# Padded tiles so that both operands of a split matmul start at a multiple of 128 bytes

## Chip, cores and metric

One core of a Trainium2 chip runs the kernel. The metric is device time in microseconds (us) of one execution; three runs of the kernel before gave a median of 1478.23 us (1478.17 to 1478.27).

## What is computed

A decoder layer on 256 tokens of width 2048, in float32: one input projection of 14,848 columns, retention with four heads, sliding-window attention with 32 query heads and a sink, two gates, an output projection, a layer norm, a SwiGLU feed-forward of width 5632 and a second layer norm. Cut to what matters here:

```python
proj = h @ w_in[l]
...
merged = jax.nn.sigmoid(gate_a) * ret + jax.nn.sigmoid(gate_b) * att
h = layer_norm(DEEPNORM_ALPHA * h + merged @ w_out[l], ln1_g[l], ln1_b[l])
ffn = (jax.nn.silu(h @ w_gate[l]) * (h @ w_up[l])) @ w_down[l]
h = layer_norm(DEEPNORM_ALPHA * h + ffn, ln2_g[l], ln2_b[l])
```

## The kernel before

**Split matmuls.** Every large product is done in the type `float32r`. Each float32 operand is split into a rounded high part and the rest: ScalarE casts a weight block `raw` to `wh` (L188), VectorE subtracts to get `wl` (L189), and three matmuls per tile stand for one (L204 to L206):

```python
nc.tensor.matmul(self.acc[t], lhsT=xh, rhs=wh[:, j], start=st, stop=False)
nc.tensor.matmul(self.acc[t], lhsT=xh, rhs=wl[:, j], start=False, stop=False)
nc.tensor.matmul(self.acc[t], lhsT=xl, rhs=wh[:, j], start=False, stop=sp)
```

`lhsT` is the stationary operand: 128 columns, loaded by an LDWEIGHTS of its own that the profile books on PEld. `rhs` is the moving operand: 512 columns. There is one LDWEIGHTS for each matmul, and it is issued one matmul ahead. Names as the profile prints them: `acc<-wh,xh` is moving `wh`, stationary `xh`.

**Stages.** The class `Chunk` walks one block of 512 output columns over all k; `Stream` puts the chunks behind each other and starts loads and casts ahead. In order of time:

- input projection, 29 chunks of 16 k-tiles by two token tiles, stationary `xh`/`xl` (the split input). The first chunk (moving `wh1`/`wl1` in the code, printed as `wh`/`wl`) loads the input along with its weights. Attention, retention and gates run between its steps as background jobs: transposes (L492), scores (L539, L606) and values (L568, L632), all plain float32 matmuls;
- output projection, 4 chunks, stationary `mh`/`ml`; then the first layer norm;
- gate and up projection: two chunks (`Chunk`, L204 to L206), then ten `PairChunk`s (L294 to L296), stationary `hh`/`hl`. A `PairChunk` also uses sums of its operands: stationary `sh`/`sl`, moving `th`/`tl`. In each, three groups of 12 matmuls with moving `th`/`tl` stand between groups with moving `wh`/`wl`;
- down projection in three parts, 12 chunks, stationary `ph`/`pl`, placed after every fourth `PairChunk` or so; then the second layer norm and the store.

The order on each engine is the order of the code: `Stream.run` issues one step of matmuls, then `pump` lets background jobs go one step.

**Where tiles lie.** Tile pools take SBUF as two stacks, a left one that grows up and a right one (`side=RIGHT`) that grows down from the top; each tile is rounded up to 32 bytes per partition and nothing else aligns it. The left stack begins at 16512 bytes, a multiple of 128. `const` puts 1056 bytes (`cst`) and 32 (`halfpi`) there, so everything behind it is 64 bytes off a multiple of 128; in `xp` three tables of 1088 bytes bring `xh` and what follows back to a multiple. The right stack begins 32 bytes under the top, so all its tiles, whose sizes are multiples of 128, start 96 bytes past a multiple. That gives, from the layout of the built program, in bytes past a multiple of 512:

| operands (moving / stationary) | split matmuls | before | after |
|---|---|---|---|
| `wh1`,`wl1` / `xh`,`xl` (first chunk) | 96 | 32 / 0 | 0 / 384 |
| `wh`,`wl` / `xh`,`xl` | 2304 | 192 / 0 | 384 / 384 |
| `wh`,`wl` / `mh`,`ml` | 384 | 192 / 480 | 384 / 384 |
| `wh`,`wl` / `hh`,`hl`,`sh`,`sl` | 1662 | 192 / 192 | 384 / 384 |
| `th`,`tl` / `hh`,`hl`,`sh`,`sl` | 360 | 480 / 192 | 384 / 384 |
| `wh`,`wl` / `ph`,`pl` | 1056 | 192 / 480 | 384 / 384 |

The step from one slice of a tile to the next (`wh[:, j]`, `xh[:, k]`, a token tile) is a multiple of 512 bytes, so a tile has one such value for all its slices.

Of the kernel before, what the change touches and what calls it, by code (L numbers as in the profile page):

```python
# [9 lines left out]
F32 = mybir.dt.float32  # L10
F32R = mybir.dt.float32r
I32 = mybir.dt.int32
AF = mybir.ActivationFunctionType
ALU = mybir.AluOpType
RIGHT = "right"

P = 128
# [36 lines left out]
    "215db93af8c88f39c4105f38a7072d37"  # L54
)
NFR = 136


def _split_const(v, grid, parts):
# [34 lines left out]
def layer_kernel(ctx, tc, a, out):  # L94
    nc = tc.nc
    PS = bass.MemoryType.PSUM

    const = ctx.enter_context(tc.tile_pool(name="const", bufs=1))
    rawp = ctx.enter_context(tc.tile_pool(name="raw", bufs=3))
    spl = ctx.enter_context(tc.tile_pool(name="spl", bufs=NSPL))  # L100
    psc = ExitStack()
# [37 lines left out]
    class Chunk:  # L139
# [25 lines left out]
        def dma(self, b):  # L165
            k, n = self.blocks[b]
            if self.src is None:
                x_dma(b)
                self.raw[b] = xraw[b][:, :, SEQ:]
                return  # L170
            r = rawp.tile([P, KB, C], F32, name="raw")
            if n == KB:
                nc.sync.dma_start(out=r, in_=self.src[k // KB])
            else:
                o = k % KB
                nc.sync.dma_start(out=r[:, 0:n], in_=self.src[k // KB][:, o:o + n])
            self.raw[b] = r
# [175 lines left out]
    jobs = {}  # L353

    NC0 = P + NFR
    cst = const.tile([P, NC0], F32, name="cst")
    ident = cst[:, 0:P]
    freq = cst[:, P:NC0]
    halfpi = const.tile([P, 1], F32, name="halfpi")
    nc.gpsimd.memset(halfpi, math.pi / 2)  # L360

    def bcast_cols(dram, c0, n):
# [13 lines left out]
    xp = inp.enter_context(tc.tile_pool(name="xp", bufs=1))  # L376
# [1 line left out]
    dmask = msk[:, 0:RH * 384].rearrange("p (h c) -> p h c", h=RH)  # L378
    bmask = msk[:, RH * 384:]
    sinks = xp.tile([P, NH], F32, name="sinks")  # L380
    cosr = xp.tile([P, 2, NFR], F32, name="cosr")
    sinr = xp.tile([P, 2, NFR], F32, name="sinr")
    sinn = xp.tile([P, 2, NFR], F32, name="sinn")
    xh = xp.tile([P, KT, SEQ], F32R, name="xh")
    xl = xp.tile([P, KT, SEQ], F32R, name="xl")
    att = xp.tile([P, 2, DM], F32, name="att")
# [5 lines left out]
    ini = isc.enter_context(tc.tile_pool(name="ini", bufs=1))  # L392
# [9 lines left out]
    xraw = {}  # L402

    def x_dma(b):
        k = sum(XS[:b])
        r = ini.tile([P, max(XS), SEQ + C], F32, name="xraw", bufs=XB)
        nc.sync.dma_start(out=r[:, 0:XS[b]], in_=a["xw"][:, k:k + XS[b]])
        xraw[b] = r
        if b == 2:
            nc.scalar.dma_start(out=cst, in_=a["consts"][:, 0:NC0])  # L410
            xraw["pos"] = ini.tile([P, 2], I32, name="posi")
            nc.scalar.dma_start(out=xraw["pos"], in_=a["pos"])

    def x_cast(b):
# [9 lines left out]
    def tables():  # L424
        posi = xraw["pos"]
        posf = ini.tile([P, 2], F32, name="posf")
        nc.vector.tensor_copy(out=posf, in_=posi)
        ang = ini.tile([P, 2, NFR], F32, name="ang")
        for t in range(2):
            nc.vector.tensor_scalar(out=ang[:, t], in0=freq, scalar1=posf[:, t:t + 1], scalar2=None, op0=ALU.mult)  # L430
        yield
        SH = [P, 2, NFR]
        cur = ang
# [40 lines left out]
        yield  # L474

    def rot_small(x16, t, n):
        # x16: [P, n, 2, 8]
        sh = [P, n, 2, 8]
        t1 = ap_.tile([P, n, 2, 8], F32, name="ra")
        t2 = ap_.tile([P, n, 2, 8], F32, name="rb")  # L480
        cs = cosr[:, t, 128:136].unsqueeze(1).unsqueeze(1).broadcast_to(sh)
        sp = sinr[:, t, 128:136].unsqueeze(1).broadcast_to([P, n, 8])
        sn = sinn[:, t, 128:136].unsqueeze(1).broadcast_to([P, n, 8])
        nc.vector.tensor_mul(out=t1, in0=x16, in1=cs)
        nc.vector.tensor_mul(out=t2[:, :, 0], in0=x16[:, :, 1], in1=sn)
        nc.vector.tensor_mul(out=t2[:, :, 1], in0=x16[:, :, 0], in1=sp)
        nc.vector.tensor_add(out=x16, in0=t1, in1=t2)
# [12 lines left out]
    def akv_bg():  # L500
        for _ in range(AKD):
            yield
        for t in range(2):
            rot_small(kvt[:, t, 0:256].rearrange("p (h d) -> p h d", d=HD)[:, :, 0:16].rearrange("p h (a b) -> p h a b", a=2), t, NKV)
            kd = ap_.tile([P, NKV, 2, HD], F32, name="kd")
            kv_ = kvt[:, t, 0:256].rearrange("p (h d) -> p h d", d=HD)
            for u in range(2):
                nc.vector.tensor_copy(out=kd[:, :, u], in_=kv_)
            yield
            ps = transpose4([kd[:, g].rearrange("p a d -> p (a d)") for g in range(NKV)])  # L510
            yield
            nc.scalar.copy(out=kT[:, :, t * P:(t + 1) * P], in_=ps)
            yield
# [5 lines left out]

    def attention(g, t, q):  # L520
        rot_small(q.rearrange("p (h d) -> p h d", d=HD)[:, :, 0:16].rearrange("p h (a b) -> p h a b", a=2), t, 8)
        yield
        ps = transpose4([q[:, i * P:(i + 1) * P] for i in range(4)])
# [157 lines left out]
    n = 0  # L681
# [12 lines left out]
        inchunk(n, lambda ch, t, j=j: gate(ch, t, j, "b")); n += 1  # L694
    mark_b = len(stream.steps)

    # out projection
    sc = {}

    def lhs_m(k, t):  # L700
# [178 lines left out]
            stream.add(Chunk([a["w_down"][c, f0 + b] for b in range(nk // KB)], nk, lhs_p, lambda ch, t, part=part, c=c: done_d(ch, t, part, c),  # L879
                             order=stagger(NSPL) if part == 2 and c == 3 else None))  # L880

    # ---- run
    i = 0
    for b, n in enumerate(XS):
        stream.precast[i] = lambda b=b: x_cast(b)
# [27 lines left out]
    hp = fsc.enter_context(tc.tile_pool(name="hp", bufs=1))  # L913
# [5 lines left out]
    sc["hl"] = hp.tile([P, KT, SEQ], F32R, name="hl")  # L919
    sc["sh"] = hp.tile([P, 4, NQ, P], F32R, name="sh")  # L920
    sc["sl"] = hp.tile([P, 4, NQ, P], F32R, name="sl")
    sc["stats"] = hp.tile([P, 2, 4, 6], F32, name="stats1")
    nc.sync.dma_start(out=sc["hres"], in_=a["x"].rearrange("(t p) d -> p t d", p=P))
    gains = {}
    for nm in ("ln1_g", "ln1_b"):
# [13 lines left out]
    psc.close()  # L939
    p8 = ctx.enter_context(tc.tile_pool(name="p8", bufs=8, space=PS, reuse_waits="tile"))  # L940
    psp["all"] = p8
    sc["stats"] = hp.tile([P, 2, 4, 6], F32, name="stats2")
    stream.run(mark_e, PC)
    for nm, tg in (("ln2_g", "hh"), ("ln2_b", "hl")):
        gains[nm] = hp.tile([P, DM], F32, name=tg)
# [79 lines left out]
```

## Time and profile before

| | us |
|---|---|
| median of three runs | 1478.23 |
| span of the profiled execution, first to last instruction | 1476.8 |
| TensorE busy in it | 1460.0 (99%) |
| VectorE busy | 962.6 (65%) |
| ScalarE busy | 654.7 (44%) |
| granted TensorE clock, mean | 0.996 of full |

The profile records the span of its execution and no total beside it; 1.4 us lie between the span and the median of the runs. A matmul's end is modelled in the profile and neighbours overlap in it (one of 0.39 us starts every 0.23 us), so what a matmul costs is read from the distance between two starts, which is called its pace here. A busy TensorE alone doesn't say whether it could go faster.

### The profile page before, as it was taken

How to read it: one execution, taken by the hardware profiler on the slowest of the kernel's cores; microseconds unless marked ns; L12 is line 12 of the kernel's file. 1: busy time of each engine (PE TensorE's matmuls, PEld its weight loads, DVE VectorE, ACT ScalarE, POOL GpSimd, SP SyncE). 2: the span in 40 equal slices, each digit the busy share in tenths (PEclk: the TensorE clock that was granted, in tenths of full speed). 3: DMA queues.
4: the chain of work that ended last, by engine and by line, in shares of the span. 5: the costliest groups of instructions: out<-in, count | busy, mean ns of one | idle time of the engine just before them, and what ended most of it. 6: DMA issues, size and time to landing. Idle time of an engine off the chain costs nothing.

```text
span 1476.8 us, 15948 instructions
## 1 busy us (share of the span) xinstructions
PE 1460.0 (99%) x6562; PEld 1177.8 (80%) x6562; DVE 962.6 (65%) x1011; ACT 654.7 (44%) x617; POOL 0.9 (0%) x6
## 2 busy tenths in 40 slices
PE   8999999999999999999999999999999999999997
PEld 6878888878788787788877888888888888888885
DVE  8455555454555545555598887457998755798756
ACT  6464543343443434443354554344455433454431
POOL 0000000000000000000000000000000000000000
PEclk9999999999999999999999999999999999999998
DMA  8643334555555455575455555555555555655561
GB/s 295 234 145 125 115 115 143 197 176 186 181 201 173 172 197 172 179 276 208 163 183 205 186 206 190 174 196 199 206 194 190 188 192 182 217 185 214 193 222 69
DMA packets 40232, 274.73 MB, mean 186 GB/s; under 512 B 4704, under 2 KB 4832, under 8 KB 8160
## 3 DMA queue, kind: packets, MB, share of 16 engines
q1 hardware_dynamic: 39296, 272.53, 52.6%
q10 hardware_dynamic: 864, 1.19, 0.2%
q8 instruction: 51, 0.84, 0.2%
q14 instruction: 21, 0.17, 0.0%
HBM read 271.60 MB, written 2.10 MB: 185 GB/s over the span
## 4 chain that ended last, share of the span: by engine, by line
PE 97%; DVE 2%; DMA 0%; issue 0%; ACT 0%; DVEq 0%; ACTq 0%
PE acc L204 15%; PE acc L206 15%; PE acc L205 15%; PE bank L294 9%; PE bank L296 9%; PE bank L295 9%; PE bank L204 6%; PE bank L206 6%; PE bank L205 6%; PE tr L492 2%; PE mx L568 1%; PE mx L539 1%; DVE wl L189 1%; PE bank L492 1%; PE mx L632 0%; DVE hres L724 0%
## 5 line engine op out<-in xcount | busy, mean ns | idle before, releaser
L189 DVE TENSOR_TENSOR wl<-raw,wh 128x2048 fp32r<-128x2048 f32 x164 | 375.7, 2291 | 318.7 <-ACT wh L188 318.3
L188 ACT CAST wh<-raw 128x2048 fp32r<-128x2048 f32 x164 | 313.2, 1910 | 454.5 <-PE acc L206 249.9
L204 PE MATMUL acc<-wh,xh 128*128 128x512 f32 x800 | 321.5, 403 | 1.8 <-ACT wh L188 1.8
L205 PE MATMUL acc<-wl,xh 128*128 128x512 f32 x800 | 318.9, 399 | 0.5 <-DVE wl L189 0.5
L206 PE MATMUL acc<-wh,xl 128*128 128x512 f32 x800 | 317.4, 397 | 0.0
L274 ACT CAST wh<-raw 128x1536 fp32r<-128x1536 f32 (+1 forms) x80 | 140.4, 1755 | 129.5 <-PE bank L296 78.5
L275 DVE TENSOR_TENSOR wl<-raw,wh 128x1536 fp32r<-128x1536 f32 (+1 forms) x80 | 166.5, 2088 | 26.7 <-ACT wh L274 25.9
L204 PEld LDWEIGHTS acc<-wh,xh 128*128 128x128 f32 x800 | 150.8, 189 | 40.3 <-ACT wh L188 3.2
L205 PEld LDWEIGHTS acc<-wl,xh 128*128 128x128 f32 x800 | 150.7, 188 | 37.6 <-issue 2.2
L294 PE MATMUL bank<-wh,hh 128*128 128x512 f32 x460 | 180.4, 392 | 0.0
L206 PEld LDWEIGHTS acc<-wh,xl 128*128 128x128 f32 x800 | 150.6, 188 | 37.4 <-issue 1.3
L296 PE MATMUL bank<-wh,hl 128*128 128x512 f32 x460 | 179.3, 390 | 0.0
L295 PE MATMUL bank<-wl,hh 128*128 128x512 f32 x460 | 178.9, 389 | 0.0
L204 PE MATMUL bank<-wh,ph 128*128 128x512 f32 x352 | 139.5, 396 | 0.0
L206 PE MATMUL bank<-wh,pl 128*128 128x512 f32 x352 | 139.2, 395 | 0.0
L205 PE MATMUL bank<-wl,ph 128*128 128x512 f32 x352 | 139.2, 395 | 0.0
L296 PEld LDWEIGHTS bank<-wh,hl 128*128 128x128 f32 x460 | 86.3, 188 | 18.8
L295 PEld LDWEIGHTS bank<-wl,hh 128*128 128x128 f32 x460 | 86.4, 188 | 18.2
L294 PEld LDWEIGHTS bank<-wh,hh 128*128 128x128 f32 x460 | 86.3, 188 | 17.9
L274 ACT CAST th<-tsum 128x2048 fp32r<-128x2048 f32 x30 | 57.5, 1915 | 53.8 <-DVE tsum L262 34.9
L275 DVE TENSOR_TENSOR tl<-tsum,th 128x2048 fp32r<-128x2048 f32 x30 | 68.8, 2292 | 16.0 <-ACT th L274 16.0
L206 PEld LDWEIGHTS bank<-wh,pl 128*128 128x128 f32 x352 | 66.1, 188 | 16.0
(187 smaller groups left out, 1489.0 us busy)
## 6 DMA issues: line engine op xcount, KB each, us to landing
raw<-in_w_in SPq DMA_DIRECT2D x96, 1024.0 KB, 4.9
raw<-in_w_gu SPq DMA_DIRECT2D x88, 1024.0 KB, 5.0
raw<-in_w_down SPq DMA_DIRECT2D x44, 1024.0 KB, 5.0
raw<-in_w_out SPq DMA_DIRECT2D x16, 1024.0 KB, 5.0
xraw<-in_xw SPq DMA_DIRECT2D x7, 768.0 KB, 5.7
hres<-in_x SPq DMA_DIRECT2D x1, 2048.0 KB, 7.6
gg<-in_gn_g SPq DMA_DIRECT2D x4, 256.0 KB, 3.7
gb<-in_gn_b SPq DMA_DIRECT2D x4, 256.0 KB, 3.7
```

The source lines that it names most:

```text
L188: nc.scalar.copy(out=h[:, 0:m], in_=r)
L189: nc.vector.tensor_sub(out=l[:, 0:m], in0=r, in1=h[:, 0:m].bitcast(F32))
L204: nc.tensor.matmul(self.acc[t], lhsT=xh, rhs=wh[:, j], start=st, stop=False)
L205: nc.tensor.matmul(self.acc[t], lhsT=xh, rhs=wl[:, j], start=False, stop=False)
L206: nc.tensor.matmul(self.acc[t], lhsT=xl, rhs=wh[:, j], start=False, stop=sp)
L274: nc.scalar.copy(out=h_, in_=r)
L275: nc.vector.tensor_sub(out=l_, in0=r, in1=h_.bitcast(F32))
L294: nc.tensor.matmul(self.acc[p], lhsT=xh, rhs=wh[:, j], start=st, stop=False)
L295: nc.tensor.matmul(self.acc[p], lhsT=xh, rhs=wl[:, j], start=False, stop=False)
L296: nc.tensor.matmul(self.acc[p], lhsT=xl, rhs=wh[:, j], start=False, stop=sp)
L492: nc.tensor.transpose(ps[:, i], s, ident)
L539: nc.tensor.matmul(sps[u][:, i], lhsT=qT[u * HD:(u + 1) * HD, h // 2], rhs=kT[u * HD:(u + 1) * HD, g, 0:W], start=True, stop=True)
```

## The change

No instruction is added, removed or moved, and no wait is: both programs have the same 9,143 instructions in the same order with the same waits. Tiles of odd width get padding, so that every later tile of a pool starts at a multiple of 128 bytes: `cst` 264 to 288 columns, `halfpi` 1 to 32, the three rotary tables 136 to 144 columns, `posi` 2 to 32, the statistics of the layer norms 6 to 8 columns. A tile `edge` of 96 bytes that nobody uses is put at the top of the right stack. Three Sin activations now write 2x136 where they wrote 272 elements, and four BN_AGGR read 4x6 where they read 24.

```diff
+LINE = 32
+NFL = 144
...
     const = ctx.enter_context(tc.tile_pool(name="const", bufs=1))
+    edge = ctx.enter_context(tc.tile_pool(name="edge", bufs=1, side=RIGHT))
+    edge.tile([P, LINE - 8], F32, name="edge")
...
-    cst = const.tile([P, NC0], F32, name="cst")
+    cst = const.tile([P, LINE * -(-NC0 // LINE)], F32, name="cst")
...
-    halfpi = const.tile([P, 1], F32, name="halfpi")
+    halfpi = const.tile([P, LINE], F32, name="halfpi")[:, 0:1]
...
-    cosr = xp.tile([P, 2, NFR], F32, name="cosr")
-    sinr = xp.tile([P, 2, NFR], F32, name="sinr")
-    sinn = xp.tile([P, 2, NFR], F32, name="sinn")
+    cosr = xp.tile([P, 2, NFL], F32, name="cosr")[:, :, 0:NFR]
+    sinr = xp.tile([P, 2, NFL], F32, name="sinr")[:, :, 0:NFR]
+    sinn = xp.tile([P, 2, NFL], F32, name="sinn")[:, :, 0:NFR]
...
-            nc.scalar.dma_start(out=cst, in_=a["consts"][:, 0:NC0])
-            xraw["pos"] = ini.tile([P, 2], I32, name="posi")
+            nc.scalar.dma_start(out=cst[:, 0:NC0], in_=a["consts"][:, 0:NC0])
+            xraw["pos"] = ini.tile([P, LINE], I32, name="posi")[:, 0:2]
...
-    sc["stats"] = hp.tile([P, 2, 4, 6], F32, name="stats1")
+    sc["stats"] = hp.tile([P, 2, 4, 8], F32, name="stats1")[:, :, :, 0:6]
...
-    sc["stats"] = hp.tile([P, 2, 4, 6], F32, name="stats2")
+    sc["stats"] = hp.tile([P, 2, 4, 8], F32, name="stats2")[:, :, :, 0:6]
```

Two comment lines are dropped as well, and the added lines shift the numbers of the lines behind them.

## Rows read from the trace of the kernel before

**Rows 1.** The page's busy time of each engine, and engines of the chain.

```profile
PE 1460.0 (99%) x6562; PEld 1177.8 (80%) x6562; DVE 962.6 (65%) x1011; ACT 654.7 (44%) x617; POOL 0.9 (0%) x6
...
PE 97%; DVE 2%; DMA 0%; issue 0%; ACT 0%; DVEq 0%; ACTq 0%
```

**Rows 2.** Waits of TensorE: line, releaser, us in total, times, longest.

```profile
PE acc L204 <- ACT wh L188: 1.8, 1, 1.8
...
PE acc L205 <- DVE wl L189: 1.0, 2, 0.5
```

**Rows 3.** Groups of matmuls by shape: count, busy us, mean ns, idle us.

```profile
L206 PE MATMUL acc<-wh,xl 128*128 128x512 f32 x800 | 317.4, 397 | 0.0
...
L296 PE MATMUL bank<-wh,hl 128*128 128x512 f32 x460 | 179.3, 390 | 0.0
...
L206 PE MATMUL bank<-wh,pl 128*128 128x512 f32 x352 | 139.2, 395 | 0.0
...
L206 PE MATMUL acc<-wh,ml 128*128 128x512 f32 x128 | 50.6, 395 | 0.0
...
L296 PE MATMUL bank<-th,sl 128*128 128x512 f32 x90 | 35.6, 395 | 0.0
...
L296 PE MATMUL bank<-th,hl 128*128 128x512 f32 x30 | 11.9, 397 | 0.0
...
L296 PE MATMUL bank<-wh,sl 128*128 128x512 f32 x30 | 11.7, 389 | 0.0
```

**Rows 4.** The same groups from 420 to 460 us, in the input projection.

```profile
L205 PE MATMUL acc<-wl,xh 128*128 128x512 f32 x58 | 22.9, 396 | 0.0
L206 PE MATMUL acc<-wh,xl 128*128 128x512 f32 x58 | 22.9, 396 | 0.0
L204 PE MATMUL acc<-wh,xh 128*128 128x512 f32 x57 | 22.5, 395 | 0.0
```

**Rows 5.** The same groups from 762 to 788 us, in the up projection's `Chunk`.

```profile
L205 PE MATMUL acc<-wl,hh 128*128 128x512 f32 x39 | 15.2, 389 | 0.0
L206 PE MATMUL acc<-wh,hl 128*128 128x512 f32 x39 | 15.2, 389 | 0.0
L204 PE MATMUL acc<-wh,hh 128*128 128x512 f32 x38 | 14.8, 389 | 0.0
```

**Rows 6.** Timeline of TensorE in a `PairChunk`: start us, us, instruction.

```profile
802.60 0.39 PE L294 MATMUL bank<-wh,hh 128*128 128x512 f32 x1
...
804.41 0.39 PE L296 MATMUL bank<-wh,sl 128*128 128x512 f32 x1
804.64 0.40 PE L294 MATMUL bank<-th,sh 128*128 128x512 f32 x1
...
807.21 0.40 PE L296 MATMUL bank<-th,hl 128*128 128x512 f32 x1
807.44 0.40 PE L294 MATMUL bank<-wh,hh 128*128 128x512 f32 x1
...
809.07 0.39 PE L295 MATMUL bank<-wl,hh 128*128 128x512 f32 x1
```

**Rows 7.** Timeline of TensorE around eight transposes, next `PairChunk`.

```profile
865.88 0.48 PE L294 MATMUL bank<-wh,hh 128*128 128x512 f32 x1
866.19 0.40 PE L295 MATMUL bank<-wl,hh 128*128 128x512 f32 x1
...
866.88 0.39 PE L295 MATMUL bank<-wl,hh 128*128 128x512 f32 x1
```

**Rows 8.** Timeline of all engines at 800 us: a matmul and the next weight load.

```profile
800.79 0.39 PE L295 MATMUL bank<-wl,hh 128*128 128x512 f32 x1
800.79 0.19 PEld L296 LDWEIGHTS bank<-wh,hl 128*128 128x128 f32 x1
```

**Rows 9.** Stretches: us, busy PE, PEld, DVE, ACT, POOL, clock, DMA share, GB/s.

```profile
9.00:42.00 33.00, 32.51 (x135) 25.81 (x134) 32.06 (x61) 22.40 (x24) 0.00 (x0) 0.96 0.86 319
42.00:648.60 606.60, 606.41 (x2830) 486.98 (x2829) 323.73 (x432) 267.23 (x335) 0.00 (x0) 1.00 0.49 168
...
742.00:790.00 48.00, 46.94 (x213) 37.47 (x212) 44.03 (x54) 23.08 (x24) 0.00 (x0) 1.00 0.56 197
792.00:916.00 124.00, 123.47 (x549) 101.18 (x548) 101.01 (x82) 61.26 (x43) 0.00 (x0) 1.00 0.55 196
```

## Prediction

> **What bounds the kernel now.** I read the page first. TensorE is busy 99% of the span and takes 97% of the chain that ended last; VectorE has 65% and ScalarE 44% [rows 1]. The view of waits says why that share is not hiding stalls: in the whole run TensorE's longest entry is one wait of 1.8 us, at the start, and the next is 1.0 us in two pieces [rows 2]. So the time is the number of matmuls times their pace, and only a change of the pace or of the count can move it by much. This change leaves the count alone.
>
> Does the pace depend on where operands lie? The trace of before holds the comparison, since its tiles lie at different offsets. By groups, a split matmul is booked with 389 to 390 ns where moving `wh` meets stationary `hl` or `sl`, and with 395 to 397 ns where `wh` meets `xl`, `ml` or `pl`, or `th` meets `sl` or `hl` [rows 3]. Ends are modelled, so I check with starts. From 420 to 460 us, 173 matmuls touch the window [rows 4]. The first may have begun up to 0.396 us before it, so their pace is about 40.4/173 = 0.2335 us. From 762 to 788 us it is 26.4/116 = 0.2275 us [rows 5]. Both stretches run at the full granted clock, the higher of the two levels [rows 9].
>
> These are different stages, so the timeline inside one `PairChunk` matters more. From the start at 802.60 to that at 804.64 are nine matmuls with moving `wh`/`wl`: 2.04/9 = 0.2267 us. From 804.64 to 807.44 are twelve with moving `th`/`tl` over the same stationary tiles: 2.80/12 = 0.2333 us [rows 6]. Neither operand alone decides. `wh` is fast with `hl` and slow with `xl`; `hl` and `sl` are fast with `wh` and slow with `th` [rows 3]. What the fast pairs share, and no slow pair has, is that moving and stationary operand start at the same offset within 512 bytes: 192 and 192, by the table of the layout. Differences of 192, 224 and 288 bytes all give the slow pace.
>
> The place where the two reads meet is seen too: the next weight load starts in the same 0.01 us as the running matmul [rows 8], so both streams walk through SBUF side by side for most of the load's 0.19 us. I read the 6.7 ns as a cost of their offset.
>
> **What the change does, term by term.** After the padding every split matmul but those of the first chunk has both operands at 384 past a multiple of 512, so the difference is zero where it is zero now and where it is not. That this exact value was never run is the main risk, priced below.
>
> *Faster pairs.* At the slow pace now: 800 x 3 with `xh`/`xl` less the 96 of the first chunk (16 k-tiles x 2 x 3), 128 x 3 with `mh`/`ml`, 352 x 3 with `ph`/`pl`, 90 x 3 and 30 x 3 with `th`/`tl` [rows 3], where each line stands for its three. That is 2304 + 384 + 1056 + 360 = 4104. In these stages the program's order has 65 places where a split matmul follows a transpose or an attention matmul; the pace of such a first one is set by the break, so 4039 remain. At 0.2333 - 0.2267 = 0.00667 us each: **26.9 us**.
>
> *Settling.* A fast pair is not fast at once after a break. After the twelve with `th`/`tl`, at 807.44, the next seven starts take 809.07 - 807.44 = 1.63 us where 7 x 0.2267 = 1.59 would do: 0.04 us lost [rows 6]. After transposes, the three from 866.19 to 866.88 take 0.69 against 0.68: 0.01 us [rows 7]. I take the middle, 0.025, for each of the 65 breaks: **1.6 us given back**. In return the 30 returns from `th` to `wh` (three in each of ten `PairChunk`s) are no break any more: 30 x 0.04 = **1.2 us gained**.
>
> *The first chunk.* Its offsets agree modulo 128 after, not modulo 512, and no pair of before shows that case. It doesn't matter much: the DMA engines are 86% busy at 319 GB/s there and VectorE is busy 32.06 of 33.00 us [rows 9], so I take 0, with 96 x 0.0067 = 0.6 us as the upper end.
>
> *What must keep up.* At the fast pace 24 matmuls, one weight block of 1 MB, take 5.44 us in place of 5.60. The input projection has VectorE busy 324 and ScalarE 267 of 607 us and DMA at 0.49 [rows 9]; the up projection's `Chunk`s already live at the fast pace with DMA at 0.56 [rows 9]. In the `PairChunk`s VectorE is busy 101 of 124 us [rows 9]; they get only 3 x 12 x 6.7 ns = 0.24 us and their share of the settling shorter in some 43 us each (the 124 us hold not quite three), under 1%, and have about 18% of idle VectorE time to take it from. So nothing is due to come late. Should a wait appear, it would be of TensorE on the `th`/`tl` casts, and the most it can undo is the 360 x 6.7 ns = 2.4 us of that group.
>
> *The padded tiles themselves.* Three Sin activations and four BN_AGGR with another shape handle the same elements, and most of them beside matmuls. I take 0. Plain float32 transposes and attention matmuls get other offsets too. I take no gain or loss for them, since nothing in the trace compares two offsets of one of them.
>
> **Sum.** 26.9 - 1.6 + 1.2 = 26.5 us. Against the profiled span: 1476.8 - 26.5 = 1450.3. The runs' median lies 1.4 us over that span, and that stays: **1451.7 us**. Its own bounds: settling at 0.04 per break and no return from `th` gives 24.3 us and 1453.9; settling at 0.01 with the first chunk's 0.6 gives 28.1 us and 1450.1. The paces of whole stretches, 0.2335 and 0.2275, hold settling already and give 4039 x 0.0060 = 24.2 us, inside by 0.1. So 1450 to 1454.
>
> **The rivals.** *No effect.* The fast pace could belong to something that goes along with the offsets in this layout. Against it stands that one stationary tile has both paces inside one `PairChunk` [rows 6], and that `wh` has both [rows 3]; for it only that no run has moved a tile yet. It gives 1478.2. [...] The two paces speak against reading it so strictly, and I leave it 7 in 100.
>
> *Slower: the offset 64 itself, not the match.* All fast pairs now start 64 past a multiple of 128 on both sides. If this value is what pays and a multiple of 128 doesn't, the forecast's 26.5 us never come, and the 1662 matched matmuls (460 x 3, 30 x 3 and 64 x 3 of the `Chunk`s) fall to 0.2333: 1662 x 0.0067 = 11.1 us lost, 1489.3 us. It decides at the first matmul with `hh`, at 742 us. For it: a stationary operand at 0 (`xl`) is slow today, and no split pair at 0 and 0 can be seen. Against it: two streams that walk side by side should feel their distance and not their common place, and `hl` at 64 is slow with `th`. 4 in 100.
>
> *Half: matched pairs don't settle among the attention jobs.* 58 of the 65 breaks lie in the input projection. The jobs give a break every 24 matmuls or so there, and if the pace needs far longer to settle after attention's many shapes than after transposes, some 18 matmuls of each such run stay slow: 58 x 18 x 0.0067 = 7.0 us less, 1458.7 us. The seven matmuls of [rows 6] are the worst that I see, so it would need more than twice that. 9 in 100.
>
> **How the numbers follow.** The forecast has 80 in 100, the half 9, no effect 7, slower 4. The range takes the forecast's bounds and the half case, with half a microsecond beyond the lower one: 1449.5 to 1460. What measurement of this kernel can tell from no change is about 0.2%, some 3 us: faster by more holds the forecast and the half case, 0.89; same 0.07; slower 0.04.
>
> **What would show it.** In the profile after, split matmuls of every group should be booked with 389 to 391 ns (the first groups of `xh` a little more for breaks and the first chunk), twelve `th` matmuls should take 2.72 us, and the stretch that now holds 173 matmuls in 40 us should hold 178. The busy time of VectorE and ScalarE should be as now, and no new wait of TensorE over 1 us should stand in the waits. A `wh`/`hh` group at 396 ns makes the forecast wrong towards the slower rival; `xh` groups that stay at 396 make it no effect; long stretches at the fast pace with short ones at the slow pace between attention jobs make it the half case.

## Result and the profile after

The median went from 1478.25 to 1452.76 us (four runs each; 1452.66 to 1452.90 after). The ratio is 0.983, with a 95% interval from 0.981 to 0.984: 25.5 us were gained where 26.5 were forecast (to 1451.7 us). The profiled execution has a span of 1450.9 us (forecast 1450.3) and took 1452.66 us, 1.8 us more.

The page of the kernel after, busy time of each engine, then the engines of the chain:

```profile
PE 1434.0 (99%) x6562; PEld 1177.6 (81%) x6562; DVE 961.8 (66%) x1011; ACT 654.1 (45%) x617; POOL 0.9 (0%) x6
...
PE 96%; DVE 3%; DMA 0%; issue 0%; ACT 0%; DVEq 0%; ACTq 0%
```

Against [rows 1], TensorE's busy time fell by 26.0 us with the same 6562 matmuls; VectorE and ScalarE did the same work in the same time. The share, 99%, didn't move at all: it can't tell matmuls that start every 0.2333 us [rows 6] from those that start every 0.2267.

Groups of matmuls by shape, in the same columns as [rows 3]:

```profile
L210 PE MATMUL acc<-wh,xl 128*128 128x512 f32 x800 | 313.2, 391 | 0.0
...
L300 PE MATMUL bank<-wh,hl 128*128 128x512 f32 x460 | 179.1, 389 | 0.0
...
L210 PE MATMUL bank<-wh,pl 128*128 128x512 f32 x352 | 137.0, 389 | 0.0
...
L210 PE MATMUL acc<-wh,ml 128*128 128x512 f32 x128 | 49.8, 389 | 0.0
...
L300 PE MATMUL bank<-th,sl 128*128 128x512 f32 x90 | 35.0, 389 | 0.0
```

The four groups that stood at 395 to 397 ns now stand at 389 to 391; `hl` was at 390 and is at 389. Nothing that was fast has lost. The 178 matmuls forecast for the 40 us from 420 can't be counted as they were, since a break has moved into that window: it holds 175 split matmuls and four transposes.

Timeline of TensorE in a `PairChunk` of the kernel after; columns as in [rows 6]:

```profile
788.80 0.39 PE L300 MATMUL bank<-wh,sl 128*128 128x512 f32 x1
789.03 0.39 PE L298 MATMUL bank<-th,sh 128*128 128x512 f32 x1
...
791.52 0.39 PE L300 MATMUL bank<-th,hl 128*128 128x512 f32 x1
791.75 0.39 PE L298 MATMUL bank<-wh,hh 128*128 128x512 f32 x1
791.97 0.39 PE L299 MATMUL bank<-wl,hh 128*128 128x512 f32 x1
792.20 0.39 PE L300 MATMUL bank<-wh,hl 128*128 128x512 f32 x1
792.43 0.39 PE L298 MATMUL bank<-wh,hh 128*128 128x512 f32 x1
```

The twelve matmuls with `th`/`tl`, from 789.03 to 791.75, take 2.72 us where they took 2.80 [rows 6], and the three behind them take 0.68: the return to `wh` is no break any more.

Where the time came from shows in the line of the third matmul: duration min/median/max in ns, then first and last start in us. Before:

```profile
L206 PE MATMUL acc<-wh,xl x800: 388/394/628, 8.0 to 648.6; 128*128 128x512 f32 x160
...
L206 PE MATMUL bank<-wh,pl x352: 392/395/397, 920.1 to 1465.7; 128*128 128x512 f32 x176
...
L206 PE MATMUL acc<-wh,ml x128: 389/395/398, 649.3 to 740.2; 128*128 128x512 f32 x128
```

After:

```profile
L210 PE MATMUL acc<-wh,xl x800: 387/389/628, 8.0 to 635.3; 128*128 128x512 f32 x160
...
L210 PE MATMUL bank<-wh,pl x352: 388/389/397, 903.5 to 1439.8; 128*128 128x512 f32 x176
...
L210 PE MATMUL acc<-wh,ml x128: 387/389/393, 636.0 to 724.6; 128*128 128x512 f32 x128
```

To the hundredth, the last split matmul of the input projection starts 13.3 us earlier (648.59 to 635.28), that of the output projection 15.5 (740.16 to 724.63, so 2.2 of its own), the last of all 25.9 (1465.71 to 1439.82, so 10.4 for the whole feed-forward part). Not all of this is pace: the second chunk starts 0.4 us earlier already (31.94 to 31.53), before any pair that got faster, 0.33 of it because the first split matmul starts earlier (6.89 to 6.56). That leaves 12.9 us to the input projection and 25.5 in all.

Waits of TensorE stay within 0.5 us of what they were. Beside [rows 2], before had a third one, which stands between the two shown there:

```profile
PE tr L399 <- POOL warm L395: 1.5, 1, 1.5
```

The longest after:

```profile
PE tr L403 <- POOL warm L399: 1.4, 1, 1.4
PE acc L208 <- ACT wh L192: 1.3, 1, 1.3
PE acc L209 <- DVE wl L193: 1.2, 2, 0.8
```

### The profile page after: what moved, and what is told of

Same layout as the page of the kernel before. It is cut to its first block, busy times and chain, and to the rows that moved or that the text cites. A ratio compares the mean times of both kernels' runs of the same rounds, so it can differ in the third digit from the quotient of the medians.

```text
span 1450.9 us, 15948 instructions
## 1 busy us (share of the span) xinstructions
PE 1434.0 (99%) x6562; PEld 1177.6 (81%) x6562; DVE 961.8 (66%) x1011; ACT 654.1 (45%) x617; POOL 0.9 (0%) x6
## 4 chain that ended last, share of the span: by engine, by line
PE 96%; DVE 3%; DMA 0%; issue 0%; ACT 0%; DVEq 0%; ACTq 0%
PE acc L208 15%; PE acc L210 15%; PE acc L209 15%; PE bank L298 10%; PE bank L300 9%; PE bank L299 9%; PE bank L210 6%; PE bank L208 6%; PE bank L209 5%; PE tr L496 2%; PE mx L572 1%; PE mx L543 1%; DVE wl L193 1%; PE bank L496 1%; PE mx L636 0%; DVE hres L728 0%
## 5 line engine op out<-in xcount | busy, mean ns | idle before, releaser
L208 PE MATMUL acc<-wh,xh 128*128 128x512 f32 x800 | 317.6, 398 | 1.3 <-ACT wh L192 1.3
L209 PE MATMUL acc<-wl,xh 128*128 128x512 f32 x800 | 314.4, 393 | 0.8 <-DVE wl L193 0.8
L210 PE MATMUL acc<-wh,xl 128*128 128x512 f32 x800 | 313.2, 391 | 0.0
```

## Experiments

The theory to test is the match: the pace depends on the distance between the starts of moving and stationary operand. The rivals are that a multiple of 128 (or of 64) itself pays, and that the gain has another cause. Every experiment edits the changed kernel by a pad tile or a slice and nothing else, so the instructions and their order stay. "Distance" is moving start minus stationary start, modulo 512. Paces in the text are means over neighbouring starts in the trace, waits left out.

**Left padding only.** One part of the change undone.

```diff
-    edge = ctx.enter_context(tc.tile_pool(name="edge", bufs=1, side=RIGHT))
-    edge.tile([P, LINE - 8], F32, name="edge")
```

> The left stack stays padded, the tile at the top of the right stack is left out, so mh, ml, ph, pl, th and tl start 96 bytes past a multiple of 128 again. Match theory: the 1800 matmuls that use them go back to a pace of 0.2333 us and the pairs with xh and hh keep 0.2267: 1452.8 + 1800 x 0.0067 + 30 x 0.04 = 1466 us, ph groups booked with 395 ns, xh groups as in the changed kernel. No-effect theory: 1452.8 us, or 1478 if the gain has another cause.

Measured: 1467.04 us, ratio 0.993 (0.991 to 0.994). Its groups by shape:

```profile
L208 PE MATMUL acc<-wh,xl 128*128 128x512 f32 x800 | 313.3, 392 | 0.0
...
L298 PE MATMUL bank<-wh,hl 128*128 128x512 f32 x460 | 179.0, 389 | 0.0
...
L208 PE MATMUL bank<-wh,pl 128*128 128x512 f32 x352 | 139.5, 396 | 0.0
...
L208 PE MATMUL acc<-wh,ml 128*128 128x512 f32 x128 | 50.7, 396 | 0.0
...
L298 PE MATMUL bank<-th,sl 128*128 128x512 f32 x90 | 35.7, 397 | 0.0
```

Exactly the groups with one operand in the right stack are back at 396 to 397 ns; `xl` and `hl` keep 392 and 389. The time is 14.3 us above the changed kernel where 13 was expected: at the distance that `ph` and `mh` have here, 416, their pace is 0.2343 us, above the 0.2333 of the sum. So 96 unused bytes in one place carry more than half of the gain, and the gain follows the operands that were moved.

**Match away from any multiple of 128.** Both stacks shifted by 32 bytes (the right one by 480 down, which is 32 up modulo 512).

```diff
-    edge.tile([P, LINE - 8], F32, name="edge")
+    edge.tile([P, LINE - 8 + 120], F32, name="edge")
...
+    const.tile([P, 8], F32, name="base")
     cst = const.tile([P, LINE * -(-NC0 // LINE)], F32, name="cst")
```

> Every tile of both stacks is moved by 32 bytes, so no operand of a split matmul starts at a multiple of 128 or of 64 any more, while moving and stationary operand still agree modulo 512 (outside the first chunk). Match theory: the same time as the changed kernel, 1452.8 us within 0.5, all groups at 389 to 391 ns. Theory that a multiple of 128 (or of 64) is itself what pays: all 5766 matmuls fall to 0.2333, 1452.8 + 5700 x 0.0067 = 1491 us.

Measured: 1453.53 us (1452.66 to 1454.53), ratio 0.983 (0.982 to 0.985). Its groups:

```profile
L210 PE MATMUL acc<-wh,xl 128*128 128x512 f32 x800 | 313.1, 391 | 0.0
...
L300 PE MATMUL bank<-wh,hl 128*128 128x512 f32 x460 | 179.1, 389 | 0.0
...
L210 PE MATMUL bank<-wh,pl 128*128 128x512 f32 x352 | 137.0, 389 | 0.0
```

The groups are those of the changed kernel, though no operand of a split matmul starts at a multiple of 64. The median is 0.8 us above the changed kernel, a little more than the half microsecond allowed: two of the four runs took 1452.66 and 1452.82 us, the other two 1454.25 and 1454.53, and no trace of these two was kept to say why. The rival's 1491 us are far off. The multiple of 128 that the change aims at is not what pays; the match is.

**Distances, first set.** Pads ahead of `xh` and `hh` and a larger `edge`.

```diff
-    edge.tile([P, LINE - 8], F32, name="edge")
+    edge.tile([P, LINE - 8 + 16], F32, name="edge")
...
+    xp.tile([P, 64], F32, name="xpad")
     xh = xp.tile([P, KT, SEQ], F32R, name="xh")
...
+    hp.tile([P, 8], F32, name="hpad")
     sc["hh"] = hp.tile([P, KT, SEQ], F32R, name="hh")
```

> All tiles start at multiples of 32 as before, but moving minus stationary is 256 bytes for xh, 64 for mh and ph, 480 for hh and sh, 416 for th (modulo 512). Match modulo 512: every pair at 0.2333 us, 1452.8 + 5700 x 0.0067 + some = 1491 us. Match modulo 256: the xh pairs (2304) keep 0.2267 and the rest falls, 1476 us. A theory that some other distance is free of any conflict would show a pace below 0.2267 in one of the four groups.

Measured: 1468.68 us, one run. Neither sum was met, for two reasons that its groups show:

```profile
L210 PE MATMUL acc<-wh,xl 128*128 128x512 f32 x800 | 312.6, 391 | 0.0
L300 PE MATMUL bank<-wh,hl 128*128 128x512 f32 x460 | 181.9, 396 | 0.0
...
L210 PE MATMUL bank<-wh,pl 128*128 128x512 f32 x352 | 138.0, 392 | 0.0
```

At 256 `xl` is as fast as at 0, so modulo 512 was too narrow. And `pl`, at 64, lies between the two levels with 392 ns and a pace of 0.229, while `hl`, at 480, is at the slow one. With `xh` fast the sum was 1476, and some 1440 matmuls at 0.229 in place of 0.2333 take 6 us more off it.

**Distances, second and third set.** The same pads in other sizes; for `xh` a slice that starts 16 bytes, then 4 bytes, into a wider tile. Of the second:

```diff
-    xh = xp.tile([P, KT, SEQ], F32R, name="xh")
+    xh = xp.tile([P, KT * SEQ + 4 * LINE], F32R, name="xh")[:, 4:4 + KT * SEQ].rearrange("p (k c) -> p k c", k=KT)
```

> Moving minus stationary (modulo 512) is 496 bytes for xh, 96 for mh and ph, 384 for hh and sh, 288 for th. After the run with 256 for xh, in which those pairs stayed at 227 ns, agreement modulo 256 is the theory: here no group agrees, so all are at 232 to 235 ns and the time is about 1452.8 + 5700 x 0.0067 = 1491 us. Rival, agreement modulo 128 (what the change aims at): the 1662 pairs with hh and sh (384 is three times 128) stay at 227 ns and the time is 1480 us. A fine dependence, on the distance within 16 or 32 bytes, would show in xh (496, that is 16 bytes short) as a pace between 227 and 233.

> Moving minus stationary (modulo 512) is 508 bytes for xh (one element short), 448 for mh and ph, 160 for hh and sh, 224 for th. Agreement modulo 256 to the byte: all groups at 232 to 235 ns, about 1491 us. Rival: what counts is a line of 16 bytes or more, so that one element's distance costs little and xh stays near 227 ns: about 1476 us. The 64 bytes of the earlier run gave 229 ns for ph; 448 is the same distance the other way, and 229 there would mean that the size of the distance counts, 233 that its direction does.

Measured: 1484.31 and 1486.91 us, one run each, below the 1491 expected, since some distances cost 5 to 6 ns on the mean and not the full 6.7. The groups of the second set:

```profile
L210 PE MATMUL acc<-wh,xl 128*128 128x512 f32 x800 | 317.3, 397 | 0.0
L300 PE MATMUL bank<-wh,hl 128*128 128x512 f32 x460 | 181.5, 395 | 0.0
```

`hl` at 384, three times 128, is slow: agreement modulo 128 isn't enough. `xl` is slow on the mean at 496 and, in the third set, at 508, where one element of 4 bytes separates the starts (pace 0.2324). `pl` at 448 in the third set is at 0.2333, so 64 one way isn't 64 the other way. Sixty matmuls lie between the two starts of each pair of lines of the third set, and they take 13.94 and 14.00 us:

```profile
430.60 0.40 PE L208 MATMUL acc<-wh,xh 128*128 128x512 f32 x1
...
444.54 0.39 PE L208 MATMUL acc<-wh,xh 128*128 128x512 f32 x1
...
940.20 0.39 PE L208 MATMUL bank<-wh,ph 128*128 128x512 f32 x1
...
954.20 0.39 PE L208 MATMUL bank<-wh,ph 128*128 128x512 f32 x1
```

The mean for `xh` at 496 hides two paces. Each stretch between two breaks settles at one of them and keeps it: of the 31 stretches of 24 or more matmuls behind the first chunk, nine are at 0.2267 us, the pace of a match, and 22 at 0.2332 to 0.2336, with the same offsets and a granted clock of 1.00 in both. Thirty matmuls of one stretch and thirty of a later one, in the second set, take 6.80 and 7.00 us:

```profile
488.28 0.39 PE L208 MATMUL acc<-wh,xh 128*128 128x512 f32 x1
...
495.08 0.39 PE L208 MATMUL acc<-wh,xh 128*128 128x512 f32 x1
...
500.29 0.40 PE L208 MATMUL acc<-wh,xh 128*128 128x512 f32 x1
...
507.29 0.40 PE L208 MATMUL acc<-wh,xh 128*128 128x512 f32 x1
```

In the changed kernel and with `xh` at 256 all 31 stretches settle at 0.2267. So a match makes every stretch fast, while at another distance a stretch may happen to be; what picks its pace, no run shows.

**Distances, fourth set.** `xpad` of 448, `hpad` of 192 and `edge` of 128 bytes more.

> Moving minus stationary (modulo 512) is 64 bytes for xh, 128 for mh and ph, 320 (64 modulo 256) for hh and sh, 192 for th. Agreement modulo 256 with a halfway level at 64: xh and hh pairs at 229 ns, mh and ph at 232 to 233, th at 233: 1452.8 + 3966 x 0.0024 + 1800 x 0.0065 = 1474 us. Rival, the 229 ns seen for ph at 64 belonged to that stage alone: xh and hh at 233 ns, 1490 us. If 128 is as good as 0 after all, mh and ph stay at 227 ns, about 1464 us.

Measured: 1472.43 us, one run. `xh` at 64 has a pace of 0.230, `hh` at 320 has 0.229, `ph` at 128 has 0.232: the level between belongs to the distance and not to a stage. Here, too, 0.230 is a mean of two paces: 29 of the 31 stretches settle at 0.229, two of 249 matmuls each at 0.2333. Sixty matmuls of one of these two, then sixty of another stretch, take 14.00 and 13.73 us:

```profile
430.19 0.40 PE L208 MATMUL acc<-wh,xh 128*128 128x512 f32 x1
...
444.19 0.40 PE L208 MATMUL acc<-wh,xh 128*128 128x512 f32 x1
...
610.28 0.39 PE L208 MATMUL acc<-wh,xh 128*128 128x512 f32 x1
...
624.01 0.39 PE L208 MATMUL acc<-wh,xh 128*128 128x512 f32 x1
```

The booked duration of `xl` is 395 ns in this run, as at the slow pace, so between the two levels only starts tell the distances apart. Mean paces over all runs, ordered modulo 256:

| distance mod 256 | pace, ns | where |
|---|---|---|
| 0 | 226.7 to 227.4 | all pairs after the first chunk in the changed kernel; `xh` at 256 |
| 32 | 233 to 234 | `th` at 288, before and in the second set |
| 64 | 229 to 230 | `ph` at 64; `xh` at 64 (two paces); `hh` at 320 |
| 96 | 233 to 234 | `ph`, `th` at 96 |
| 128 | 232 to 233 | `hh` at 384; `ph` at 128 |
| 160 | 234 | `hh` at 160; `ph` at 416 |
| 192, 224 | 233 | `xh`, `ph` before; `ph` at 448; `hh` at 480 |
| 240, 252 | 232 | `xh` at 496 (two paces) and 508 |

**First chunk matched too.** A pad so that `wh1`/`wl1` agree with `xh`.

```diff
+    ini.tile([P, 96], F32, name="wpad")
```

> The changed kernel with 384 bytes of padding ahead of wh1 and wl1, so that the first chunk, too, agrees modulo 512 with xh. If 128 bytes apart costs as much as any other distance, its pairs go from 233 to 227 ns; the chunk lives on the loads, so the time stays within 0 to 0.6 us of 1452.8: 1452.5. If agreement modulo 128 is enough, nothing changes in the pace either.

Measured: 1452.34 us (1452.24 to 1452.40, four runs), ratio 0.982 (0.981 to 0.984), the best of all kernels run: 0.4 us under the changed kernel, whose runs lie all above it. The chunk's pairs went from 0.233 to 0.228 us, and from its first matmul to that of the next chunk it takes 24.56 us in place of 24.97. At a distance of 128 they had been slow in the changed kernel.

## Why the prediction was right

**The bound.** Right: a kernel that is nothing but matmuls back to back got faster by their pace, 25.5 of the 25.9 us of span, and no wait of TensorE grew by more than 0.2 us. One line of the waits was passed over: the second longest is the 1.5 us for `warm`, not the 1.0 us that the prediction names. It stands ahead of the first split matmul and changes nothing in the argument.

**The faster pairs, 26.9 us.** Right in place and nearly in size. The reading that neither operand alone decides, drawn from one `PairChunk`, carried it, and left padding alone confirmed it from the other side. Seen by stages, the forecast's 2246 pairs of the input projection (2304 less 58) at 6.7 ns, less settling, are 13.5 us, for 12.9 measured behind the first chunk; `mh` has 384 x 0.0067 = 2.6 for 2.2 measured; the feed-forward part, with the returns from `th`, 1416 x 0.0067 + 1.2 = 10.6 for 10.4. Most of the 0.6 us in the input projection is a count: a break takes two distances out of the pace, and the prediction took out one for each. The distance from the first to the second matmul behind a break (0.31 us in [rows 7]) has a median of 0.320 us before and 0.317 after there, and 57 such distances at 6.7 ns are 0.4 us.

**Settling, 1.6 us.** Right: from the starts after, the pairs behind the breaks lose 0.026 us each on average (0.010 to 0.047 for eight of ten), 1.8 us over the 71 breaks that no wait blurs; 0.025 was taken. In the input projection's stretches of 24 or more matmuls the last distance over 0.228 us is at most the tenth behind the break. So long runs of the fast pace were reached among the attention jobs, too, and the half case did not come.

**What must keep up.** Right: TensorE's waits after are 1.4 us and less, all in places where they stood before, and none is on the `th`/`tl` casts.

**The sum** was 1.0 us too large a gain: 26.5 against 25.5, between medians and by pace alike, from the terms just named. The span fell by 25.9, since the profiled execution of before began its first split matmul late. The 1.4 us outside the span were no term of one execution: they set the span of one beside the median of others. Every run whose own span is on record takes 1.8 us over it, before (1478.24 and 1476.4) and after (1452.66 and 1450.9). So the span of 1476.8 was some 0.4 us longer than usual, the 1.4 that much too small, and in the forecast of 1451.7 the two cancel.

**The first chunk** was taken at 0, since its pairs agreed modulo 128 alone. They stayed slow, as taken, and matching them in a further run gave 0.4 us, inside the 0.6 that stood as the upper end.

**The rivals.** *No effect* fell with the result, and with left padding only, where the booked means went from 389 back to 396 and 397 ns for just those operands that were moved back. The *slower* rival, that a start 64 past a multiple of 128 pays, fell with the result too: the pairs with `hl` stay at 389 ns with both starts at 384. Start addresses do not leave TensorE's speed alone here: the same instructions at other offsets ran 25.5 us faster. Whether the weight load and the moving read meet at all, and why a distance of 0 or 256 is best, no run here shows; it wasn't tried to take the weight loads away. The link to them, and the prediction's two streams that walk side by side, are the author's estimate, argued from the common start of matmul and load, both at 800.79 us [rows 8].

One step of the reading was too narrow and did no harm: agreement modulo 512 was taken, though before, with its one matched distance of 0, could not tell 512 from 256; 256 is enough, by the one run with `xh` at 256. And the change's own rule, a multiple of 128, is too weak as such: it works because the sizes of this kernel's tiles happen to bring both operands to 384 modulo 512.

## What to carry to other kernels

Where TensorE is busy throughout with one weight load per matmul, compare the pace (distance of starts) of groups with the same shape; a few per cent between them (here 0.2333 against 0.2267 us, 2.9%) can come from the tiles' starting offsets alone. In `float32r` here, make moving and stationary operand start at the same offset modulo 256 bytes (distances of 0 and 256 are the matches that were run, at 0.2267 to 0.2274 us after the first chunk; the others had means of 0.229 to 0.234), and check the built layout: rounding each tile to 128 bytes does not ensure it (`hl` at 384 was booked with 395 ns against 389), and the 96 bytes at the edge of a stack decided over 14.3 of the 25.5 us.

## What was not expected

Starts that miss each other by 4 bytes cost most of the full amount (508: 0.2324 us against 0.2274 in the same stage), and 64 costs only 0.002 to 0.003 us (0.229 to 0.230), but 448 costs the full amount (0.2333): the effect has a direction. At 496 (0.2267 and 0.2332 to 0.2336 us) and at 64 (0.229 and 0.2333) some stretches of matmuls ran at another pace than the rest, so a distance without a match does not fix one pace. At no distance did the mean over the three matmuls of a group go below 0.2267 us. What sets this pace, no run here shows.
